# RWKV state step of a hybrid layer: both units' preparation at the step's opening, the output's scaling queued half a step later

## The chip, the cores and the metric

The kernel runs on one NeuronCore of a Trainium2 chip. That core has TensorE (PE in the profile; its weight loads are PEld), VectorE (DVE), ScalarE (ACT), GpSimd (POOL) and SyncE (SP), each with an instruction queue of its own that is worked through in order, and DMA queues that move data between HBM and the on-chip memories. Here nearly all DMAs are issued from SP's queue. The metric is the device time of one execution in microseconds (us). Three runs of the kernel before gave 2098.55, 2103.36 and 2105.53 us; the median is 2103.36 us.

## The reference, cut to what matters

A residual layer over 2048 tokens of width 1024. The normed input is projected once; the projection feeds two branches. One is an RWKV7 recurrence with 8 heads of 64, the other a latent attention that keeps the 256 best keys of each query. Their outputs are concatenated, projected back and added to the input (the measured layer closes with one more rmsnorm). The part that the change touches is the RWKV branch:

```python
def step(S, inp):                      # per token, 8 heads, state S is 64 x 64
    r_t, w_t, k_t, v_t, kk_t, a_t = inp
    sa = einsum('bhij,bhj->bhi', S, -kk_t)
    S = (S * w_t[:, :, None, :]
         + sa[..., None] * (kk_t * a_t)[:, :, None, :]
         + v_t[..., None] * k_t[:, :, None, :])
    return S, einsum('bhij,bhj->bhi', S, r_t)
...
y = rwkv7_scan(r, decay, k, v, kk, a)
mu = mean(y, -1); var = mean(square(y - mu), -1)
y = (y - mu) * rsqrt(var + GN_EPS) * gn_g + gn_b
y = y + sum(r * k * r_k, -1) * v
return y * silu(gate)
```

## The kernel before

The program has three parts in time. Up to about 1000 us the input is projected and the 256 keys of each query are found. Then the RWKV recurrence (`phase_r`, called R here) and the attention (T, lines 1221 to 1329) run beside each other. Last comes the output projection (W, lines 1362 to 1390). Every engine's order is fixed at build time by a scheduler that simulates a time line and always takes the ready instruction of the best priority: the chain of R has the highest, what stands in `with e.later()` a lower one, T lower still, W the lowest. `tc.issue_after(ins)`, in R through `behind(ins)`, puts the instructions of a block that run on the engine of `ins` behind `ins` in that engine's queue.

R works through 16 steps n of 128 tokens, each of two halves (o = 0 and 1) of 64 tokens. For one step there are two units i of four heads each. What a step needs is made two steps ahead and passes through these stages:

- `prep(n, i)`: the load `ld<-d_rw` (L937), a scan and products on DVE (L950 to L967), ACT exponentials, 16 small matmuls on PE (L974), masked into tile E by DVE (L977), the sum r*k*r_k on PE (L982) and its product with v, tile `bv`, on DVE (L984; eight buffers). POOL scales BK (L987).
- `systems`: from E of both units four stores to DRAM (`du<-E`, L1015, two from each unit) and one load of 512 KB that repeats the result over the partitions (`A<-du`, L1017). Tile A has one buffer.
- `inverse`: on POOL, Xr is set (L1025, L1027), and 31 pairs of operations (L1031 Xtmp, L1033 Xr) invert the small triangular systems in A; then a store `dx<-Xr` (L1034) and four loads `TT<-dx` (L1038; two buffers).
- `prep2`: PE transposes and ACT copies (L996 to L1006).
- `chain(n, o)`: PE reads the state with X and E (L1051, L1059), solves with TT (L1068, L1086), makes the state's change (L1093); DVE adds it into the state S (L1096), DVE makes SP, the decayed state (L1080), and ACT copies y (L1097).
- `tail_norm`: mean and variance of y in tile gst (DVE L1104 to L1111, ACT L1109), the reciprocal root as a `pow` on POOL (L1112), and the product of y with it on DVE (L1113, "the scale" below).
- `tail_out`: PE transposes y (L1120), ACT scales it into yo (L1126), POOL adds bv and multiplies by the gate gr (L1128, L1129), and yo is stored (L1130).

In step n the program opens with the inverse of step n+1, whose last L1033 is called `first`; then the norm of step n-1's y, its pow queued behind `first`; then unit 0's preparation for step n+2, its DVE work behind S of the half before; then chain half 0; then `prep2`, unit 1's preparation behind S of half 0, and `systems` for step n+2; then chain half 1 and the `tail_out` of step n-1. The scheduler fills the gaps with the matmuls, exponentials and masks of T.

Of the kernel before, what the change touches and what calls it, by code (L numbers as in the profile page):

```python
# [14 lines left out]
OP = mybir.AluOpType  # L15
# [871 lines left out]
def phase_r(env):  # L887


    e = NS(env)  # L890
    nc, tc, pa, ps, dma, V, S, G, PE, f32, rpow, nm, ident = (
        e.nc, e.tc, e.pr, e.psr, e.dma, e.V, e.S, e.G, e.PE, e.f32, e.rpow, e.nm, e.ident)
# [3 lines left out]
    NU = 2 * NC  # L896
# [4 lines left out]
    def tl(shape, dt, tag, bufs=1):  # L901
        return pa.tile(shape, dt, name=nm(tag), tag=tag, bufs=bufs)
# [105 lines left out]
    def systems(us):  # L1008

        du = e.dram([2, 2, NU, 32, 32], F32, nm("du"))  # L1010
        A = tl([128, 32, 32], F32, "A")
        for i, u in enumerate(us):
            for k in range(2):
                ps_ = slice(64 * i + k * 32, 64 * i + k * 32 + 32)
                dma(du[i, k].rearrange("u s t -> s u t"),  # L1015
                    u.E[ps_, :, :, k * 32:k * 32 + 32].rearrange("s h c t -> s (h c) t"))
        dma(A.rearrange("l s t -> l (s t)"),  # L1017
            du.rearrange("i k u s t -> (i k u) (s t)")[None].to_broadcast([4, 32, 1024]))
        return A

    def inverse(A):

        dx = e.dram([2, 2, NU, 32, 32], F32, nm("dx"))
        Xr = tl([128, 8, 32], F32, "Xr")
        G.memset(Xr, 0.0)  # L1025
        for j in range(4):
            G.memset(Xr.rearrange("p i t -> p (i t)")[32 * j:32 * j + 32, j:256:36], 1.0)  # L1027
        tmp = tl([128, 8, 32], F32, "Xtmp")
        for s in range(31):
            m, w = s // 4 + 1, 31 - s  # L1030
            G.tensor_tensor(tmp[:, :m, :w], Xr[:, :m, s:s + 1].to_broadcast([128, m, w]),  # L1031
                            A[:, s:s + 1, s + 1:].to_broadcast([128, m, w]), op=OP.mult)
            m_ = G.tensor_tensor(Xr[:, :m, s + 1:], Xr[:, :m, s + 1:], tmp[:, :m, :w], op=OP.add)  # L1033
        dma(dx.rearrange("i k u (r j) t -> j (i k u) r t", j=4), Xr)  # L1034
        TT = tl([128, NU, 32], F32, "TT", 2)
        for i in range(2):
            for k in range(2):
                dma(TT[Q[2 * i + k]], dx[i, k].rearrange("u s t -> s u t"))  # L1038
        return TT, m_.ins
# [60 lines left out]
    def tail_norm(y):  # L1100

        yv = y.rearrange("t c (h i) -> t (c h) i", h=2)
        st = tl([128, 3, NU], F32, "gst", 2)
        V.tensor_reduce(st[:, 0], yv, axis=AX.X, op=OP.add)  # L1104
        V.tensor_scalar(st[:, 0], st[:, 0], 1.0 / 64, None, op0=OP.mult)
        bc = lambda a: a[:, :, None].to_broadcast([128, NU, 64])
        V.tensor_tensor(yv, yv, bc(st[:, 0]), op=OP.subtract)
        sq = tl([128, NU, 64], F32, "ysq")
        S.activation(sq, yv, AF.Square)  # L1109
        V.tensor_reduce(st[:, 1], sq, axis=AX.X, op=OP.add)  # L1110
        V.tensor_scalar(st[:, 1], st[:, 1], 1.0 / 64, 64e-5, op0=OP.mult, op1=OP.add)  # L1111
        m = G.tensor_tensor(st[:, 2], st[:, 1], e.mhalf[:, :NU], op=OP.pow)  # L1112
        V.tensor_tensor(yv, yv, bc(st[:, 2]), op=OP.mult)  # L1113
        return m.ins

    def tail_out(us, y):

# [20 lines left out]
    def behind(ins):  # L1138
        return tc.issue_after(ins) if ins else ExitStack()

    def begin(n):
        return NS(dict(n=n, eC=tl([128, 2, NC], F32, "eC", 4), us=[]))
# [4 lines left out]
    first = G.memset(eLs[0][:, :, 0:1], 1.0).ins  # L1147
# [10 lines left out]
    y0, b0, state = None, None, None  # L1158
    for n in range(N):
        b = batch.pop(n)  # L1160
        new = batch[n + 2] = begin(n + 2) if n + 2 < N else None
        nx = batch.get(n + 1)
        with e.later():
            if nx:
                nx.TT, first = inverse(nx.A)
            if b0:
                with behind(first):
                    tail_norm(y0)
            if new:
                with behind(state):  # L1170
                    new.us.append(prep(n + 2, 0, new.eC, first))
        y = tl([128, NC, 128], F32, "y", 2)
        state = chain(b.us, b.TT, b.eC, y, n, 0)
        with e.later():
            if nx:
                for u in nx.us:
                    prep2(u)
            if new:
                with behind(state):
                    new.us.append(prep(n + 2, 1, new.eC, first))  # L1180
                new.A = systems(new.us)
        state = chain(b.us, b.TT, b.eC, y, n, 1)
        with e.later():
            if b0:
                tail_out(b0.us, y0)
        y0, b0 = y, b
    with e.later():
        tail_norm(y0)
        tail_out(b0.us, y0)


# [228 lines left out]
```

## Time and profile before

| | |
|---|---|
| median of three runs | 2103.36 us (2098.55 to 2105.53) |
| profiled execution | 2104.7 us, of which the span of the trace is 2102.9 us |
| mean granted clock of TensorE | 0.906 |
| busy: PE, DVE, ACT, POOL | 1803.3, 1296.7, 1019.8, 795.3 us |
| HBM traffic | 262.50 MB, 125 GB/s on average |

The three parts have different limits, so shares over the whole span say little. What is read below are stretches: from 1091 to 1730 us R and T run together, then R ends, and from 1830 us there is only T and then W. The stretches of the window rows are cut at the moments at which an inverse on POOL ends, so each of them is one turn of R.

### The profile page before, as it was taken

What the parts mean: (1) busy time and instruction counts of PE and PEld (TensorE: products, weight loads), DVE (VectorE), ACT (ScalarE), POOL (GpSimd) and SP (SyncE); (2) the same over time, 40 slices, a digit from 0 to 9 for tenths busy, and PEclk for the clock granted to TensorE, in tenths of its full rate; (3) what the DMA queues carried; (4) which work ended last, traced back from release to release, by engine and by line L of the source; (5) the groups of instructions that cost most, each with busy time, mean ns of one, the idle gap of its engine ahead of it and who ended that gap; (6) DMA issues with size and microseconds to landing.
All of it is one profiled execution on the core that took longest, in us unless ns stands there. A gap on an engine that the chain in (4) does not pass through costs nothing.

```text
span 2102.9 us, 36153 instructions
## 1 busy us (share of the span) xinstructions
PE 1803.3 (86%) x12906; PEld 1421.8 (68%) x12906; DVE 1296.7 (62%) x3050; ACT 1019.8 (48%) x1966; POOL 795.3 (38%) x1925
## 2 busy tenths in 40 slices
PE   5788998879796988986788988886988889899998
PEld 4666877658575867765566766665766667587776
DVE  5532538979779698986656557564756654644432
ACT  4422494453444744441355555454655567643431
POOL 1110124353544354562445645654546650100000
PEclk9778999989798999998799998798988899999999
DMA  7526334332262434234844355343454324744223
GB/s 248 199 94 200 108 101 135 101 115 85 75 239 63 135 107 136 91 95 125 204 102 105 95 136 147 105 119 98 115 143 131 93 78 108 233 128 128 66 93 112
DMA packets 309038, 262.50 MB, mean 125 GB/s; under 512 B 82544, under 2 KB 258288, under 8 KB 307696
## 3 DMA queue, kind: packets, MB, share of 16 engines
q1 hardware_dynamic: 304464, 248.03, 40.1%
q0 software_dynamic: 4384, 12.06, 1.8%
q8 instruction: 104, 1.70, 0.4%
q14 instruction: 86, 0.70, 0.1%
HBM read 166.37 MB, written 97.85 MB: 126 GB/s over the span
## 4 chain that ended last, share of the span: by engine, by line
PE 23%; POOL 14%; DMA 12%; issue 5%; DVE 4%; SPq 1%; ACT 1%; POOLq 0%; DVEq 0%; ACTq 0%
DMA A<-du 6%; POOL Xr L1033 6%; POOL Xtmp L1031 5%; PE om L1304 3%; PE po L1381 3%; PE po L1382 3%; PE po L1384 3%; PE tr L1295 3%; DMA dx<-Xr 2%; PE s L1261 2%; PE s L1262 1%; DMA TT<-dx 1%; DMA ld<-d_rw 1%; POOL yo L1129 1%; POOL gst L1112 1%
## 5 line engine op out<-in xcount | busy, mean ns | idle before, releaser
L577 PE MATMUL pm<-xh,wh 128*128 128x512 f32 x800 | 330.4, 414 | 20.3 <-DVE t L588 11.8
L578 PE MATMUL pm<-xl,wh 128*128 128x512 f32 x800 | 327.0, 409 | 0.0
L579 PE MATMUL pm<-xh,wl 128*128 128x512 f32 x800 | 326.1, 408 | 0.0
L1263 DVE CUSTOM_DVE_ANT_0 sc<-s,mk 128x512 f32<-128x512 f32 (+3 forms) x320 | 187.9, 607 | 102.8 <-PE s L1262 76.0
L1297 ACT ACTIVATE pt<-tr 128x512 f32<-128x512 f32 (+1 forms) x288 | 157.9, 569 | 160.8 <-PE tr L1295 115.9
L1031 POOL TENSOR_TENSOR Xtmp<-Xr,A 128x60 f32<-128x60 f32 (+24 forms) x496 | 146.9, 296 | 225.8 <-DMA A<-du 181.8
L577 PEld LDWEIGHTS pm<-xh,wh 128*128 128x128 f32 x800 | 158.1, 198 | 61.7 <-DVE t L588 13.7
L1270 ACT ACTIVATE sc<-sc,mx 128x128 f32<-128x128 f32 (+15 forms) x128 | 153.0, 1198 | 63.0 <-DVE mx L1269 62.7
L1295 PE MATMUL tr<-ident,sc 128*128 128x128 f32 x1088 | 180.1, 292 | 3.0 <-ACT pt L1297 2.6
L579 PEld LDWEIGHTS pm<-xh,wl 128*128 128x128 f32 x800 | 157.3, 197 | 36.4
L578 PEld LDWEIGHTS pm<-xl,wh 128*128 128x128 f32 x800 | 158.0, 197 | 35.4
L1304 PE MATMUL om<-pt,vt 128*64 128x128 f32 x2176 | 174.0, 295 | 6.2 <-DVE ga L1287 6.2
L1261 PE MATMUL s<-kt,q 128*128 128x512 f32 (+2 forms) x320 | 144.2, 454 | 35.8 <-DVE mx L1263 32.2
L1033 POOL TENSOR_TENSOR Xr<-Xr,Xtmp 128x60 f32<-128x60 f32 (+24 forms) x496 | 151.3, 305 | 37.4
L1304 PEld LDWEIGHTS om<-pt,vt 128*64 128x64 f32 x2176 | 134.2, 146 | 37.6 <-issue 19.6
L1295 PEld LDWEIGHTS tr<-ident,sc 128*128 128x128 f32 x1088 | 133.5, 149 | 33.9 <-issue 11.4
L317 ACT ACTIVATE mk<-x,st 128x1920 bf16<-128x1920 f16 (+5 forms) x72 | 98.0, 1361 | 103.6 <-POOL st L314 103.6
L249 ACT ACTIVATE rl<-lg,wi 128x512 f32<-128x512 f32 (+3 forms) x152 | 94.0, 631 | 99.6 <-PE lg L247 53.1
L1262 PE MATMUL s<-kt,q 128*128 128x512 f32 (+2 forms) x320 | 123.3, 389 | 8.1 <-DMA q<-d_q 8.0
L320 DVE TENSOR_SCALAR_CACHE_REDUCE mk<-x,st 128x2048 bf16<-128x2048 f16 (+5 forms) x72 | 120.6, 1675 | 1.4
L254 DVE SCALAR_TENSOR_TENSOR xs<-rl,wi,xs 128x512 f32<-128x512 f32 (+3 forms) x108 | 73.5, 681 | 60.9 <-ACT rl L249 60.1
L1387 POOL TENSOR_TENSOR st<-st 128x1 f32<-128x1 f32 x16 | 3.1, 195 | 277.1 <-ACT po L1386 277.1
(329 smaller groups left out, 3937.7 us busy)
## 6 DMA issues: line engine op xcount, KB each, us to landing
wraw<-in_w_in_dram SPq DMA_DIRECT2D x42, 512.0 KB
d_rw<-t SPq DMA_DIRECT2D x80, 256.0 KB
ld<-d_rw SPq DMA_DIRECT2D x32, 640.0 KB
q<-d_q SPq DMA_DIRECT2D x128, 128.0 KB
d_q<-t SPq DMA_DIRECT2D x32, 256.0 KB
d_kt<-t SPq DMA_DIRECT2D x32, 256.0 KB
kt<-d_kt SPq DMA_DIRECT2D x32, 256.0 KB
A<-du SPq DMA_DIRECT2D x16, 512.0 KB
```

The costliest lines, as they stand in the source:

```text
L577: PE.matmul(pm, wh[:, k], XH[g][:, k], start=k == 0, stop=False)
L578: PE.matmul(pm, wh[:, k], XL[g][:, k], start=False, stop=False)
L579: PE.matmul(pm, wl[:, k], XH[g][:, k], start=False, stop=k == KD - 1)
L1031: G.tensor_tensor(tmp[:, :m, :w], Xr[:, :m, s:s + 1].to_broadcast([128, m, w]), A[:, s:s + 1, s + 1:].to_broadcast([128, m, w]), op=OP.mult)
L1033: m_ = G.tensor_tensor(Xr[:, :m, s + 1:], Xr[:, :m, s + 1:], tmp[:, :m, :w], op=OP.add)
L1261: PE.matmul(pS[:, :wp], qh[:, h, qs], k[:, h, :wp], start=True, stop=False)
L1262: PE.matmul(pS[:, :wp], ql[:, h, qs], k[:, h, :wp], start=False, stop=True)
L1263: V.tensor_tensor_reduce(out=rows[h][:, c0:c0 + w], in0=pS[:, :w], in1=mk[:, c0:c0 + w], scale=1.0, scalar=LOW, op0=OP.add, op1=OP.max, ac ...
L1270: marks[p, b] = S.activation(rows[h][:, :n], rows[h][:, :n], AF.Exp, bias=mx[:, h, 4:5], accum_out=sums[:, h:h + 1]).ins
L1295: PE.transpose(pt[:, i, h], rows[h][:, (kb + i) * 128:(kb + i) * 128 + 128], ident)
L1297: S.activation(w[:, :m], pt[:, :m], AF.Copy)
L1304: PE.matmul(po[HALF[h]], v[:, (kb + i) % 4, HALF[h]], w[:, i, h], start=kb + i == 0, stop=kb + i == b)
```

## The change

The preparation of both units for step n+2 and its `systems` are now written at the step's opening, both behind S of the half before; unit 1 stood behind S of half 0 until now. `tail_norm` returns its last operation, the scale, without running it; the scale is written after chain half 0 and queued on DVE behind that half's S. The pow is the same operation on the same engine, behind the same instruction, called through a helper (`rpow`). No operation is added or removed, and the arithmetic is the same.

```diff
@@ -1109,9 +1109,8 @@
         S.activation(sq, yv, AF.Square)
         V.tensor_reduce(st[:, 1], sq, axis=AX.X, op=OP.add)
         V.tensor_scalar(st[:, 1], st[:, 1], 1.0 / 64, 64e-5, op0=OP.mult, op1=OP.add)
-        m = G.tensor_tensor(st[:, 2], st[:, 1], e.mhalf[:, :NU], op=OP.pow)
-        V.tensor_tensor(yv, yv, bc(st[:, 2]), op=OP.mult)
-        return m.ins
+        rpow(st[:, 2], st[:, 1])
+        return lambda: V.tensor_tensor(yv, yv, bc(st[:, 2]), op=OP.mult)
 
     def tail_out(us, y):
 
@@ -1165,27 +1164,28 @@
                 nx.TT, first = inverse(nx.A)
             if b0:
                 with behind(first):
-                    tail_norm(y0)
+                    scale = tail_norm(y0)
             if new:
-                with behind(state):
-                    new.us.append(prep(n + 2, 0, new.eC, first))
+                for i in range(2):
+                    with behind(state):
+                        new.us.append(prep(n + 2, i, new.eC, first))
+                new.A = systems(new.us)
         y = tl([128, NC, 128], F32, "y", 2)
         state = chain(b.us, b.TT, b.eC, y, n, 0)
         with e.later():
+            if b0:
+                with behind(state):
+                    scale()
             if nx:
                 for u in nx.us:
                     prep2(u)
-            if new:
-                with behind(state):
-                    new.us.append(prep(n + 2, 1, new.eC, first))
-                new.A = systems(new.us)
         state = chain(b.us, b.TT, b.eC, y, n, 1)
         with e.later():
             if b0:
                 tail_out(b0.us, y0)
         y0, b0 = y, b
     with e.later():
-        tail_norm(y0)
+        tail_norm(y0)()
         tail_out(b0.us, y0)
 
 
```

Since the scheduler sets the order from these priorities, the change moves rows on all engines. Three places of the two built programs are shown; a row is line, operation, output<-inputs with the numbers of the buffers, and the shape.

First place: step 3, on DVE, around the S of its half 0 (`S_1345`). SP_9430 belongs to half 1, y and gst to step 2's norm; ld, BK, X and E belong to unit 1 for step 5. Before:

```order
L1096 TENSOR_TENSOR S_1345_7771<-ch_9315,SP_9282 64x4x64 x2
L950 SCALAR_TENSOR_TENSOR L_9372<-restart_7748,ld_9368 128x256
L959 TENSOR_TENSOR BK_9378<-ld_9368 128x4x64
L962 TENSOR_SCALAR ka_9380<-ld_9368,kac,oka 128x128 x2
L1080 TENSOR_TENSOR SP_9430<-S_1345_7771,eC_8399 64x256 x2
L1280 TENSOR_TENSOR rs_15052<-sums_14898,rs_15052 128x2
L963 TENSOR_TENSOR ld_9368<-ld_9368,ka_9380 128x256
L966 TENSOR_TENSOR X_9377<-ld_9368,eL_1347_7775 128x4x64
L967 TENSOR_TENSOR X_9377<-ld_9368,eL_1347_7775 128x4x64
L1113 TENSOR_TENSOR y_8896<-y_8896,gst_9216 128x512
...
L977 TENSOR_TENSOR E_9388<-rp_9389,mask_7751 128x512
L977 TENSOR_TENSOR E_9388<-rp_9390,mask_7751 128x512
```

The same place after:

```order
L1096 TENSOR_TENSOR S_1345_7771<-ch_9361,SP_9328 64x4x64 x2
L977 TENSOR_TENSOR E_9285<-rp_9286,mask_7751 128x512
L1269 TENSOR_REDUCE mx_14897<-mx_14897 128x1
L1080 TENSOR_TENSOR SP_9430<-S_1345_7771,eC_8399 64x256 x2
L1113 TENSOR_TENSOR y_8942<-y_8942,gst_9216 128x512
L977 TENSOR_TENSOR E_9285<-rp_9287,mask_7751 128x512
L984 TENSOR_TENSOR bv_9302<-rp_9300,vt_9266 128x256
```

Unit 1's scan and products stood between S and the scale and its E far behind the scale; now they all stand ahead of S, except the second half of E, which stands right behind the scale.

The same step on SP, from the store dx of the inverse for step 4 to the load A for step 5 (the two du are unit 1's). Before:

```order
L1034 DMA dx_9140<-Xr_9141 4x256x32
L1038 DMA TT_9211<-dx_9140 32x8x32 x4
L941 DMA vt_9739<-d_v 128x2x192
L1329 DMA d_y<-ga_14633 128x128
L1221 DMA kt_15387<-d_kt_68 64x2x512
L1221 DMA kt_15387<-d_kt_69 64x2x512
L1244 DMA ga_15305<-d_ga 128x128
L1015 DMA du_9408<-E_9388 32x8x32 x2
L1221 DMA kt_15662<-d_kt_68 64x2x512
L937 DMA ld_9738<-d_rw 128x10x128
L1017 DMA A_9409<-du_9408 128x1x1024
```

The same place after:

```order
L1034 DMA dx_9140<-Xr_9141 4x256x32
L1242 DMA mk_15176<-d_mask_72 128x256
L1038 DMA TT_9211<-dx_9140 32x8x32 x4
L1015 DMA du_9305<-E_9285 32x8x32 x2
L937 DMA ld_9635<-d_rw 128x10x128
L1017 DMA A_9306<-du_9305 128x1x1024
```

A still stands behind TT and behind the du of unit 1, but fewer loads of T stand in between.

Second place: SP around the load A for step 7 (A_10149 before, A_10046 after) and the TT of step 6 (dx_9880, TT_9951). Before:

```order
L1015 DMA du_10148<-E_10128 32x8x32 x2
L1034 DMA dx_9880<-Xr_9881 4x256x32
L937 DMA ld_10478<-d_rw 128x10x128
L1017 DMA A_10149<-du_10148 128x1x1024
L1038 DMA TT_9951<-dx_9880 32x8x32 x4
```

The same place after:

```order
L1034 DMA dx_9880<-Xr_9881 4x256x32
...
L1038 DMA TT_9951<-dx_9880 32x8x32 x4
L1015 DMA du_10045<-E_9985 32x8x32
L937 DMA ld_10335<-d_rw 128x10x128
L1232 DMA q_2764_15667<-d_q_66 64x2x256
L1232 DMA q_2765_15670<-d_q_67 64x2x256 x2
L1329 DMA d_y<-ga_15178 128x128
L1242 DMA mk_15673<-d_mask_79 128x1152
L1244 DMA ga_15520<-d_ga 128x128
L1015 DMA du_10045<-E_10025 32x8x32 x2
L937 DMA ld_10375<-d_rw 128x10x128
L1017 DMA A_10046<-du_10045 128x1x1024
```

A stood ahead of TT and now stands behind TT, unit 1's du, two ld and five other entries.

Third place: POOL within the inverse for step 4 (A_9039 before, A_8936 after), where the yo of step 1 is finished. Before:

```order
L1031 TENSOR_TENSOR Xtmp_9147<-Xr_9141,A_9039 128x3x23
L1128 TENSOR_TENSOR yo_9123<-yo_9123,bv_8010 128x256
L1033 TENSOR_TENSOR Xr_9141<-Xr_9141,Xtmp_9147 128x3x23
L1128 TENSOR_TENSOR yo_9131<-yo_9131,bv_8050 128x256
L1129 TENSOR_TENSOR yo_9123<-yo_9123,gr_9124 128x256
L1031 TENSOR_TENSOR Xtmp_9147<-Xr_9141,A_9039 128x3x22
L1129 TENSOR_TENSOR yo_9131<-yo_9131,gr_9132 128x256
L1033 TENSOR_TENSOR Xr_9141<-Xr_9141,Xtmp_9147 128x3x22
```

The same place after:

```order
L1031 TENSOR_TENSOR Xtmp_9147<-Xr_9141,A_8936 128x5x14
L1127 TENSOR_TENSOR yo_9123<-yo_9123,bv_8010 128x256
L1033 TENSOR_TENSOR Xr_9141<-Xr_9141,Xtmp_9147 128x5x14
L1127 TENSOR_TENSOR yo_9131<-yo_9131,bv_8050 128x256
L1128 TENSOR_TENSOR yo_9123<-yo_9123,gr_9124 128x256
L1031 TENSOR_TENSOR Xtmp_9147<-Xr_9141,A_8936 128x5x13
L1128 TENSOR_TENSOR yo_9131<-yo_9131,gr_9132 128x256
L1033 TENSOR_TENSOR Xr_9141<-Xr_9141,Xtmp_9147 128x5x13
```

The four yo operations stood in the 9th and 10th pair of the 31 (width 23 and 22) and now stand in the 18th and 19th (width 14 and 13).

## Rows read from the trace of the kernel before

**Rows 1.** Page: the chain that ended last, by engine and by line.

```profile
PE 23%; POOL 14%; DMA 12%; issue 5%; DVE 4%; SPq 1%; ACT 1%; POOLq 0%; DVEq 0%; ACTq 0%
DMA A<-du 6%; POOL Xr L1033 6%; POOL Xtmp L1031 5%; PE om L1304 3%; PE po L1381 3%; PE po L1382 3%; PE po L1384 3%; PE tr L1295 3%; DMA dx<-Xr 2%; PE s L1261 2%; PE s L1262 1%; DMA TT<-dx 1%; DMA ld<-d_rw 1%; POOL yo L1129 1%; POOL gst L1112 1%
```

**Rows 2.** Waits, 1000 to 1820 us: total us, times, longest.

```profile
POOL Xtmp L1031 <- DMA A<-du: 181.8, 14, 18.6
...
DVE y L1113 <- POOL gst L1112: 74.0, 11, 15.6
...
PE ch L1068 <- DMA TT<-dx: 29.0, 5, 8.4
...
DVE bv L984 <- POOL yo L1128: 15.3, 5, 4.6
```

**Rows 3.** Windows: us, busy us of each engine, granted clock, DMA share.

```profile
1091.00:1730.60 639.60, 542.73 (x6260) 422.35 (x6258) 378.73 (x1159) 354.55 (x813) 357.60 (x1033) 0.89 0.44 114
1223.80:1276.50 52.70, 43.72 (x534) 33.68 (x534) 29.67 (x93) 28.02 (x69) 25.63 (x75) 0.93 0.57 149
1276.50:1322.90 46.40, 40.27 (x449) 30.51 (x450) 32.21 (x103) 26.58 (x69) 26.34 (x75) 0.82 0.50 134
1322.90:1363.40 40.50, 33.23 (x340) 26.90 (x338) 23.52 (x66) 17.93 (x43) 26.35 (x75) 0.75 0.41 106
1830.00:2045.00 215.00, 215.00 (x1365) 171.68 (x1365) 87.54 (x213) 87.49 (x166) 10.32 (x33) 0.99 0.34 106
```

**Rows 4.** Time line of SP, POOL, DVE after an inverse's end at 1276.5 us: start, us.

```profile
1281.26 1.80 SPq L1038 DMA_DIRECT2D TT<-dx  x4
1283.10 0.94 SPq L1015 DMA_DIRECT2D du<-E  x2
...
1285.50 0.74 SPq L1017 DMA_DIRECT2D A<-du  x1
...
1276.44 1.66 POOL L1112 TENSOR_TENSOR gst<-gst,mhalf 128x8 f32<-128x8 f32 x1
...
1296.28 0.40 POOL L1031 TENSOR_TENSOR Xtmp<-Xr,A 128x31 f32<-128x31 f32 x1 [13.15 <-DMA A<-du]
...
1278.13 1.52 DVE L1113 TENSOR_TENSOR y<-y,gst 128x512 f32<-128x512 f32 x1 [7.50 <-POOL gst L1112]
1279.57 0.68 DVE L977 TENSOR_TENSOR E<-rp,mask 128x512 f32<-128x512 f32 x1
```

**Rows 5.** Time line of SP, POOL, DVE after the end at 1223.8 us.

```profile
1237.71 0.55 SPq L1017 DMA_DIRECT2D A<-du  x1
...
1250.71 0.24 POOL L1031 TENSOR_TENSOR Xtmp<-Xr,A 128x31 f32<-128x31 f32 x1 [16.65 <-DMA A<-du]
...
1232.78 1.29 DVE L977 TENSOR_TENSOR E<-rp,mask 128x512 f32<-128x512 f32 x2 [1.38 <-PE rp L974]
```

**Rows 6.** Time line of SP, POOL, PE after the end at 1363.4 us.

```profile
1366.45 3.84 SPq L1017 DMA_DIRECT2D A<-du  x1
...
1372.25 3.57 SPq L1038 DMA_DIRECT2D TT<-dx  x4
...
1381.86 0.24 POOL L1031 TENSOR_TENSOR Xtmp<-Xr,A 128x31 f32<-128x31 f32 x1 [8.61 <-DMA A<-du]
...
1383.51 1.32 PE L1068 MATMUL ch<-R,TT 32*32 32x64 f32 x16 [7.47 <-DMA TT<-dx]
```

**Rows 7.** Groups by line and form, POOL then PE, 1091 to 1730.6 us: busy, mean ns.

```profile
L1128 POOL TENSOR_TENSOR yo<-yo,bv 128x256 f32<-128x256 f32 x26 | 19.5, 750 | 1.2 <-POOL Xr L1027 1.2
...
L1304 PE MATMUL om<-pt,vt 128*64 128x128 f32 x1288 | 109.8, 301 | 4.1 <-DVE ga L1287 4.1
L1295 PE MATMUL tr<-ident,sc 128*128 128x128 f32 x644 | 108.4, 295 | 1.2 <-ACT pt L1297 1.2
L1261 PE MATMUL s<-kt,q 128*128 128x512 f32 x135 | 66.3, 491 | 19.2 <-DVE mx L1263 19.2
L1262 PE MATMUL s<-kt,q 128*128 128x512 f32 x136 | 56.6, 416 | 0.1
```

## The prediction, made before the change was run

> **What bounds the kernel now.** I read the chain that ended last first, because the change touches only R and the question is whether R is on it. It is [rows 1]: beside 23% PE it holds 14% POOL and 12% DMA, and the largest lines are the load of A (6%) and the two lines of the inverse (6% and 5%). So for part of the span the end is set by a turn through POOL and the DMAs, not by TensorE. The waits of that part say where the turn stands still [rows 2]: POOL waited 181.8 us in 14 places for A. The next thing that the change names, DVE before the scale, waited 74.0 us in 11 places for POOL's pow.
>
> The windows tell how much room there is [rows 3]. From 1091 to 1730.6 us there are 14 turns of R in 639.6 us, 45.7 us each; PE is busy for 542.7 of them, so 97 us are idle. From 1830 to 2045 us PE is busy for 215.00 of 215 us: what T has left by then is paid in full. A shorter turn therefore pays only so far as PE's idle 97 us are cut, and the end time is the work of PE plus the idle time that R forces on it.
>
> A turn is 26 us of inverse (some 23 us of its own and four yo operations of 0.75 us, 3 us [rows 7]) and a gap of about 20 us until the next A has landed. I cut the 14 gaps (from the end of one inverse to the first L1031 of the next) into three kinds, of which one each is shown. On time: the inverse ends at 1276.5 us, TT is issued at 1281.26, the du of unit 1 at 1283.10, A at 1285.50, and POOL goes on at 1296.28 us, a gap of 19.8 us [rows 4]; seven are of this kind, 19.4 us on average. Late E: unit 1's E comes on DVE only at 1232.78 us, so A is issued 13.9 us after the end at 1223.8 and the gap is 26.9 us [rows 5]; three, 26.8 us on average. Early A: A goes out ahead of TT, at 1366.45 us, the gap is 18.5 us, but PE then waits 7.47 us for TT [rows 6]; four, 16.4 us on average. Seven, three and four of these make 281.8 us.
>
> **The change part by part.** Nothing is added or removed; the sum is of places.
>
> *Both preparations at the opening.* Where E was late, unit 1's scan and products stood behind S of half 0 and partly behind the stalled scale; now they stand ahead of S. Only the second half of E comes right behind the scale, as in the on-time turn, where E started at 1279.57 us, 1.44 us after the scale, and A went out 6 us later [rows 4]. So the three late gaps should become on-time ones. In the new order A stands ahead of TT in four of the 14 gaps, as before. New sum: 10 x 19.4 + 4 x 16.4 = 259.6 us, that is **-22 us** against 281.8.
>
> *SP's queue.* The early A's now lie at the two ends of R, and those in the middle are all behind their TT. In front of some stand more entries than the on-time kind has: about 9 more for step 7's A, 7 for step 12's, 5 for step 13's, one or two for steps 4 and 10. An issue on SP takes 0.45 us (TT, four in 1.80) to 0.74 us (A) [rows 4]; with 0.6 us for some 25 entries it is **+15 us** (11 to 19). It is nothing if these entries have left before the du is ready, which the on-time gap speaks against: there A is issued 0.7 us behind its predecessors with no idle time in front.
>
> *The scale.* The DVE stall in front of it does not go. The pow stays behind the end of the inverse, and in the new order two to five rows lie between S and the scale, where 11 to 38 lay. DVE's stream from one scale to the next is the same work, so the stall of 74.0 us over 11 places [rows 2] stays about what it is, and only the chain slides later against POOL. Behind the waiting scale stand E's second half, bv and T's masked scores; PE waits for the last. Price: **0**, bounds -10 to +10, since the length of the stall is the slack of the turn, 45.7 us less what DVE and PE need.
>
> *The yo operations.* The scale of step n-1 is followed by PE's transposes, ACT's yo and POOL's four yo operations, which now lie in the 18th and 19th pair of the inverse. Work of PE between the scale and the transposes is some 21.5 us (16 to 26) by the prices of rows 7, so yo is ready about 31 us after the end of the last inverse; POOL gets there at about 19.4 + 13 = 32.5 us. It just fits, and in the fuller turns it is 1 to 8 us late. I take **+5 us** for 14 turns (0 to +26). DVE's bv, which waits for an old yo to free its buffer, had 15.3 us of waits [rows 2] and goes with it.
>
> *Work of T inside R.* The scheduler believes that the new R is shorter and puts less of T into it. Counted in the order up to chain half 30, it is 5 pairs of score matmuls, 18 transposes and 26 value matmuls less. With 0.91 us a pair (491 + 416 ns), 0.168 us a transpose (108.4 / 644) and 0.17 us a value matmul (two records each, 109.8 / 1288) [rows 7] that is 4.6 + 3.0 + 4.4 = 12.0 us; at the last half 4.7 us. I take **+10 us** (5 to 13): this work is done later, where PE has no idle time [rows 3], and R is not shorter for it as long as POOL sets its pace.
>
> Sum: -22 + 15 + 0 + 5 + 10 = **+8 us**. The profiled execution took 2104.7 us, 1.3 us over the median of 2103.36; against the median the sum gives **2111 us**.
>
> **The rivals.** *A: the gain stays.* The late gaps are cured and SP's extra entries leave while DVE still works on E, so that they cost nothing; the yo operations fit. For it: the three long turns are the plainest loss in the windows, 52.7 us against 40.5 to 46.4 for the next two [rows 3]. Against it: the extra entries stand in the built order. The sum is then -22 to -27 (the waits of PE for TT, 29.0 us in 5 places [rows 2], shrink too) and 0 to +5: 2080 to 2086, say **2083 us**.
>
> *B: a loop over POOL and DVE, slower.* Scale, transposes, yo, the rest of the inverse, pow, next scale form a ring. If PE's stream from the scale to the transposes takes over 29 us rather than 21.5, every inverse stops in its 18th pair and its end, TT and pow all move. With the middle turns 2 us late each this adds 26 us in place of 5, less some that the A gap hides: +22 us or **2125 us**. For it: PE is 85% busy here, and its granted clock drops to 0.75 in single turns [rows 3]. Against it: the transposes' operands are early.
>
> *C: nothing moves.* All four terms are shifts of work against a turn that has some 5 us of slack; they cancel to within a few microseconds: **2103 us** (2099 to 2108).
>
> *D: the stall really goes.* If the half step were enough for the pow to be done when DVE comes to the scale, up to 74.0 us of DVE's waiting were freed. DVE is not what sets the turn (378.7 of 639.6 us busy [rows 3]), so at most about half would reach PE: **2070 us**. It needs the pow to run earlier, and that is still behind the inverse.
>
> *E: A's load hidden.* In the rows, A is issued 9.0 us after the end of one inverse and waited for to the last, 13.15 us of POOL standing still [rows 4]. If the earlier preparation let A go out during the inverse before, the gaps would vanish and with them most of PE's 97 us: 2104 - 97, **2006 us**. Against it: A has one buffer, which the running inverse reads to its last pair.
>
> The Trainium skill's page "DMA: Bandwidth & Descriptors" (Rules for kernel authors) asks for E's state of things: issue a DMA early, compute, wait late, so that its fixed cost overlaps. By that rule the change should gain; the trace shows the transfer fully exposed, and with one buffer it stays so.
>
> **How the numbers follow.** The forecast (2103 to 2117) gets 0.42, half of it within 0.3% of the median, which is 2097.0 to 2109.7 us and about what a measurement of this kernel can tell from no change. A gets 0.22, B 0.20, C 0.10, D 0.04, E 0.02. Faster is A, D and E: 0.28. Slower is B and over half of the forecast, 0.42. The rest, 0.30, is no change. The range of 8 in 10 runs from 2080 (most of A) to 2131 us (B with half its bound more); D and E and the edges of A and B stay out. Cases of both signs hold much of it; the likeliest one's own range is 2103 to 2117 us.
>
> **What would show it.** In the profile after: A issued within about 10 us of each inverse's end and no gap over 24 us shows the first step right; a total wait for A near 160 + 15 us shows the second; a wait of DVE for the pow still of 50 to 90 us the third (near zero: D); waits of POOL in mid-inverse for ACT's yo, 0 to 26 us, the fourth (over 1.5 us in most turns: B); PE idle in the 14 turns near 105 us and T further behind at the end of R the fifth. The forecast is wrong if the turn falls to 44 us or less (A) or rises over 47 us (B), or if PE's idle time no longer follows POOL's turn.

## The result, and the profile after

The changed kernel takes 2132.6 us (median of 4 runs, 2128.3 to 2135.6) against 2101.0 us (4 runs, 2097.7 to 2105.5) of the kernel before: a ratio of 1.0148, with a 95% interval of 1.013 to 1.0166. It is slower, as forecast, but by 31.6 us where +8 us were forecast, and it lies 1.6 us above the range. In the two profiled runs the difference is 31.0 us; these are taken apart below.

First the windows of the kernel after (columns as in [rows 3]): the same 14 turns, from the end of one inverse to the end of the 14th behind it, and all that follows.

```profile
1085.60:1743.70 658.10, 546.04 (x6108) 424.27 (x6104) 386.43 (x1137) 349.77 (x803) 371.71 (x1032) 0.87 0.43 109
1743.70:2133.90 390.20, 366.18 (x2634) 288.92 (x2632) 166.91 (x438) 177.73 (x354) 28.28 (x64) 0.96 0.40 121
```

The 14 turns start 5.4 us earlier than before (1091.0 us), take 658.1 us instead of 639.6 [rows 3], and what follows takes 390.2 us. What follows them in the kernel before:

```profile
1730.60:2102.90 372.30, 348.80 (x2452) 276.15 (x2452) 159.74 (x412) 167.05 (x335) 28.91 (x64) 0.97 0.40 123
```

So -5.4 + 18.5 + 17.9 = 31.0 us, the whole difference of the spans (2133.9 and 2102.9 us). The loss has two halves: longer turns, and more work of PE left behind them (366.2 us busy instead of 348.8).

The second half can be counted. Score matmuls, transposes and value matmuls of T from 1000 us to the end of the 14th turn, line by line, first before, then after:

```profile
L1261 PE MATMUL s<-kt,q x220: 274/476/882, 1001.8 to 1724.6; 128*128 128x512 f32 x77, 128*128 128x256 f32 x22, 128*128 128x384 f32 x11
L1295 PE MATMUL tr<-ident,sc x716: 270/273/476, 1002.8 to 1725.8; 128*128 128x128 f32 x179
L1304 PE MATMUL om<-pt,vt x1400: 272/273/476, 1013.1 to 1721.2; 128*64 128x128 f32 x175
```

```profile
L1261 PE MATMUL s<-kt,q x209: 279/478/881, 1001.9 to 1743.2; 128*128 128x512 f32 x74, 128*128 128x256 f32 x20, 128*128 128x384 f32 x11
L1295 PE MATMUL tr<-ident,sc x683: 269/273/477, 1000.9 to 1742.8; 128*128 128x128 f32 x171
L1304 PE MATMUL om<-pt,vt x1352: 272/273/477, 1008.8 to 1742.2; 128*64 128x128 f32 x194
```

11 pairs of score matmuls at 0.91 us, 33 transposes at 0.168 and 48 records of value matmuls (two make one matmul) at 0.085 [rows 7] are 19.6 us of work less, although R took longer.

The first half: cut as in the prediction, the 14 gaps are 284.4 us (before 281.7) and the 14 inverses 373.7 us (before 357.9). So 15.8 of the 18.5 us are in the inverse itself. Its two lines, busy time and mean length, before and then after:

```profile
L1033 POOL TENSOR_TENSOR Xr<-Xr,Xtmp 128x60 f32<-128x60 f32 (+24 forms) x435 | 132.8, 305 | 32.6
L1031 POOL TENSOR_TENSOR Xtmp<-Xr,A 128x60 f32<-128x60 f32 (+24 forms) x434 | 128.1, 295 | 202.5 <-DMA A<-du 163.2 <-DMA TT<-dx 7.8
```

```profile
L1033 POOL TENSOR_TENSOR Xr<-Xr,Xtmp 128x60 f32<-128x60 f32 (+24 forms) x435 | 137.9, 317 | 32.6
L1031 POOL TENSOR_TENSOR Xtmp<-Xr,A 128x60 f32<-128x60 f32 (+24 forms) x434 | 135.1, 311 | 203.6 <-DMA A<-du 172.1
```

The same operations on the same shapes are 12 and 16 ns longer, 12.1 us in sum; the four yo operations of each turn add 2.3 us (40.7 us against 38.4). The time line of POOL, then of DVE, in one inverse after shows when: the first L1033 takes 0.74 us while DVE runs L1107, the second 0.71 us while it runs L950; the L1031 between them, beside L1263, takes 0.27 us, and without DVE beside it an L1033 of 52 elements takes 0.28 us.

```profile
1682.62 0.74 POOL L1033 TENSOR_TENSOR Xr<-Xr,Xtmp 128x52 f32<-128x52 f32 x1
1683.44 0.27 POOL L1031 TENSOR_TENSOR Xtmp<-Xr,A 128x50 f32<-128x50 f32 x1
1683.79 0.71 POOL L1033 TENSOR_TENSOR Xr<-Xr,Xtmp 128x50 f32<-128x50 f32 x1
```

```profile
1682.54 0.68 DVE L1107 TENSOR_TENSOR y<-y,gst 128x512 f32<-128x512 f32 x1
1683.15 0.68 DVE L1263 CUSTOM_DVE_ANT_0 sc<-s,mk 128x512 f32<-128x512 f32 x1
...
1683.76 0.68 DVE L950 TENSOR_TENSOR_SCAN L<-restart,ld 128x256 f32<-128x256 f32 x1
```

Over all L1031 and L1033 of the 14 turns, what each is longer than the shortest of its shape in the same kernel adds up to 19.1 us before and 32.7 us after. Operations with nothing of DVE beside them carry 1.4 and 0.9 us of it (399 and 313 operations). The rest, shared out among the DVE operations beside them by the length of the overlap, is per us of overlap 0.36 to 0.44 us with L950, 0.5 with L1107, 0.2 to 0.3 with the products of `prep` (L959 to L967, without L962), and 0.02 to 0.05 with L1263 and L977, whose first input is in PSUM. Unit 1's scan and products used to run partly in the gaps, while POOL stood waiting for A; now both units' run mostly beside the inverse: the scans and products lie beside L1031 and L1033 for 57.1 us in the 14 turns, before 36.6 us, and L1107 for 8.5 us, before 1.9.

Last, the queue of SP (its waits over the same 14 turns): the rows of the yo store, L1130 before and L1129 after, and above them the longest row, T's load of ga (L1244).

```profile
SPq L1244 <- DMA d_y<-ga: 103.4, 32, 9.5
...
SPq L1130 <- POOL Xtmp L1031: 34.0, 14, 11.1
...
SPq L1130 <- POOL Xr L1033: 22.5, 12, 5.9
```

```profile
SPq L1244 <- DMA d_y<-ga: 97.8, 26, 10.3
SPq L1129 <- POOL Xtmp L1031: 56.0, 11, 17.5
SPq L1129 <- POOL Xr L1033: 43.4, 10, 14.6
SPq L1129 <- POOL yo L1128: 38.6, 5, 11.2
```

SP stands 138 us in front of these stores and waits for POOL, before 56.5 us, because yo is now made in the 16th to 22nd pair of the inverse in 11 of 13 turns, before mostly in the 1st to 11th. All that is queued behind them waits too: T's loads, ld, du. The wait for ga is about as long in both kernels; what is queued behind it differs.

### The profile page after: what moved, and what is told of

Same layout as the page of the kernel before. It is cut to its first block, busy times and chain, and to the rows that moved or that the text cites. A ratio compares the mean times of both kernels' runs of the same rounds, so it can differ in the third digit from the quotient of the medians.

```text
span 2133.9 us, 36172 instructions
## 1 busy us (share of the span) xinstructions
PE 1817.5 (85%) x12906; PEld 1431.1 (67%) x12906; DVE 1311.8 (61%) x3050; ACT 1021.5 (48%) x1966; POOL 810.0 (38%) x1925
## 4 chain that ended last, share of the span: by engine, by line
PE 21%; POOL 15%; DMA 13%; issue 4%; DVE 3%; SPq 2%; ACT 1%; POOLq 0%; DVEq 0%; ACTq 0%
POOL Xr L1033 6%; POOL Xtmp L1031 6%; DMA A<-du 6%; PE om L1304 3%; PE po L1384 3%; PE tr L1295 3%; PE po L1381 3%; PE po L1382 3%; DMA dx<-Xr 3%; PE s L1261 2%; PE s L1262 1%; DMA du<-E 1%; DMA ld<-d_rw 1%; POOL yo L1128 1%; DMA q<-d_q 1%
## 5 line engine op out<-in xcount | busy, mean ns | idle before, releaser
L1263 DVE CUSTOM_DVE_ANT_0 sc<-s,mk 128x512 f32<-128x512 f32 (+3 forms) x320 | 188.1, 605 | 129.8 <-PE s L1262 68.7
L1031 POOL TENSOR_TENSOR Xtmp<-Xr,A 128x60 f32<-128x60 f32 (+24 forms) x496 | 153.1, 309 | 226.7 <-DMA A<-du 190.4
L1261 PE MATMUL s<-kt,q 128*128 128x512 f32 (+2 forms) x320 | 147.4, 463 | 40.0 <-DVE mx L1263 34.9
L1033 POOL TENSOR_TENSOR Xr<-Xr,Xtmp 128x60 f32<-128x60 f32 (+24 forms) x496 | 156.7, 316 | 37.4
L1262 PE MATMUL s<-kt,q 128*128 128x512 f32 (+2 forms) x320 | 125.1, 394 | 11.7 <-DMA q<-d_q 11.7
```

Source lines behind the costliest of these rows:

```text
L1261: PE.matmul(pS[:, :wp], qh[:, h, qs], k[:, h, :wp], start=True, stop=False)
L1262: PE.matmul(pS[:, :wp], ql[:, h, qs], k[:, h, :wp], start=False, stop=True)
L1263: V.tensor_tensor_reduce(out=rows[h][:, c0:c0 + w], in0=pS[:, :w], in1=mk[:, c0:c0 + w], scale=1.0, scalar=LOW, op0=OP.add, op1=OP.max, ac ...
```

## The experiments

All times are medians of 4 to 12 runs beside the kernel before on the same chip, whose median there was 2098 to 2103 us. "Turns", "gaps" and "inverses" are the 14 turns cut as above, "tail" is the span behind them, transposes are the records of T's line of transposes up to their end, PE idle is the span less PE's busy time on the page. Of each edit the lines that carry it are shown; comments in them are added.

| kernel | us, ratio | turns = gaps + inverses | tail | transposes | PE idle |
|---|---|---|---|---|---|
| before | 2101, 1 | 639.6 = 281.7 + 357.9 | 372.3 | 716 | 299.6 |
| after | 2132.6, 1.0148 | 658.1 = 284.4 + 373.7 | 390.2 | 683 | 316.4 |
| part one alone | 2132.3, 1.0134 | 653.5 = 282.6 + 371.0 | 391.0 | 675 | 315.0 |
| part two alone | 2108.6, 1.0029 | 642.9 = 288.5 + 354.4 | 376.6 | 700 | 317.8 |
| stores behind dx | 2124.7, 1.0117 | 651.2 = 277.8 + 373.3 | 384.8 | 684 | 304.1 |
| E before scale | 2122.8, 1.0098 | 660.3 = 286.3 + 374.0 | 371.1 | 724 | 305.7 |
| SP free | 2126.6, 1.0141 | 645.3 = 273.5 + 371.9 | 395.2 | 676 | 311.1 |
| A before TT | 2119.2, 1.0107 | 631.2 = 254.2 + 376.9 | 394.9 | 674 | 290.2 |
| A first, SP free | 2096.6, 0.9992 | 618.5 = 244.0 + 374.6 | 393.5 | 658 | 277.1 |
| the same, no part two | 2101.3, 1.0016 | 619.8 = 246.7 + 373.1 | 395.2 | 665 | 280.9 |
| before, SP free | 2095.2, 0.9976 | 659.8 = 307.1 + 352.6 | 351.0 | 766 | 295.8 |
| before, behind A | 2095.3, 0.9959 | 661.7 = 302.3 + 359.4 | 343.1 | 774 | 305.0 |

The turn sums are single profiled executions and the scheduler rearranges T in each kernel, so differences of a few us in one column mean nothing; the interval of a ratio is given where it decides. The profiled run of "before, SP free" (2102.0 us) is the longest of its ten, that of "part two alone" (2113.1 us) the second longest.

**Which part costs.** Part one alone:

```
             if new:
-                with behind(state):
-                    new.us.append(prep(n + 2, 0, new.eC, first))
+                for i in range(2):
+                    with behind(state):
+                        new.us.append(prep(n + 2, i, new.eC, first))
+                new.A = systems(new.us)
```

> Part one alone: both units' preparation at the opening, the scale left behind the pow as before. In the built order the four yo operations stand in the 17th to 21st pair of the inverse as in the changed kernel, but unit 1's E no longer stands behind the scale in most turns. If the loss comes from the preparation's new place (yo late in the inverse, less of T inside R): 2125 to 2140 us, like the changed kernel. If it comes from the scale that is queued ahead of E (theory: PE waits for E and bv, 45.6 us in the changed kernel against 20.8 before): 2095 to 2110 us.

2132.3 us, ratio 1.0098 to 1.0171. The place of the preparation alone costs all that the change costs. PE waits 50.9 us for E and bv there too, although the scale was not moved.

Part two alone, the scale behind S of half 0 with the preparation as before:

```
             if b0:
+                with behind(state):
+                    scale()
```

> Part two alone: the scale queued behind S of half 0, the preparation as before. Its built order is that of the kernel before in the first seven turns, and yo stays in the first 12 pairs. If the loss comes from the preparation's new place: 2098 to 2110 us, no change. If it comes from the late scale itself: 2120 to 2135 us. T has 13.6 us less work inside R up to half 30 by the order, so up to +13 us is open even then.

2108.6 us, ratio 1.0012 to 1.0046: a loss that is small but clear of noise (6 us by the ratio, 7.9 by the medians), with the inverse at its old length (354.4 us) and less of T in R (700 transposes). In company with part one it adds nothing that can be measured.

**SP's queue.** First the stores alone, behind the store dx of the inverse in which yo is made:

```
+        with behind(stored[-1]):        # the DMA dx
+            for dst, yo in outs:
+                dma(dst, yo)
```

> The changed kernel with the two yo stores of each step queued on SP behind the store dx of the inverse in which yo is made; the orders of the other engines stay nearly the same. Theory of SP's queue: the stores hold SP for 138 us in the 14 turns against 64 us before, and the loads behind them come late; then this gives back 15 to 30 us (2103 to 2117 us) and SP's wait for yo is near 0. Theory of the E behind the scale, or of the inverse itself: within 5 us of the changed kernel, 2128 to 2138 us.

2124.7 us, ratio 1.0079 to 1.0155, some 8 us below the changed kernel, with intervals that overlap. It did not take the hold away, as the waits of SP show (L1123 is the load of gr):

```profile
SPq L1123 <- POOL Xtmp L1031: 72.4, 13, 17.4
SPq L1123 <- POOL Xr L1033: 68.9, 13, 14.7
```

The load of the gate gr for the next step waits for the same yo operations to free its buffer. So both were moved:

```
+            for u in us:
+                u.gr = tl([128, 2, W], F32, "gr", 2)
+                dma(u.gr, ...)           # behind dx as well
```

> The changed kernel with both the two yo stores and the two loads of gr, whose buffer is freed by the same yo operations, queued on SP behind the store dx. The earlier run moved the stores alone and the loads of gr then held SP for 141 us in the 14 turns, so SP's hold was not taken away there. Theory of SP's hold: here neither waits for POOL, T's loads come in time, and the time falls to 2108 to 2118 us. Against it: four more entries stand between dx and A in every turn, 2.4 us by 14 turns, 34 us at most; and if SP's hold costs nothing, 2125 to 2150 us.

2126.6 us, ratio 1.0105 to 1.0177. The turns fell by 13 us, the tail rose by 5. The interval overlaps that of the changed kernel (1.013 to 1.0166) almost wholly, and the expected 2108 to 2118 us did not come: SP's hold alone is not the cause of the loss.

**E behind the scale.**

```
-                with behind(state):
+                with behind(state), behind(new.us[1].made if new else state):   # made: unit 1's E
                     scale()
```

> The changed kernel with the scale queued behind unit 1's E on DVE too, so that no E stands behind the waiting scale. Theory of the E behind the scale: PE's waits for E and bv fall from 45.6 us to about 20, the time to 2105 to 2115 us; T has 16 us more work inside R up to half 30 by the order, which pulls the same way. Theory of SP's queue or of yo late in the inverse: no gain, 2128 to 2140 us, since yo stands as late or later.

2122.8 us, ratio 1.0069 to 1.0127: 10 us back. DVE's wait for the pow fell from 80.1 to 52.2 us, PE's for E and bv fell from 45.7 to 26.2 us in all, not quite to the expected 20. The longest rows are:

```profile
DVE y L1113 <- POOL gst L130: 52.2, 11, 7.8
...
DVE bv L984 <- POOL yo L1127: 31.7, 8, 8.1
PE rp L974 <- DVE bv L984: 10.9, 3, 5.1
PE rp L982 <- DVE E L977: 9.5, 7, 4.1
```

The turns did not get shorter (660.3 us); the 10 us come from T, whose 724 transposes and tail of 371.1 us are those of the kernel before. In most of these turns E is done 2 to 8 us before the inverse ends, and A still goes out 9 to 12 us after it.

**A behind TT.** In the changed kernel the longest gap is 27.0 us, from 1313.7 us. SP's time line there is the second place of the order shown ahead of the prediction:

```profile
1313.73 0.58 SPq L1034 DMA_DIRECT2D dx<-Xr  x1
1314.41 2.12 SPq L1232 DMA_DIRECT2D q<-d_q  x1
1316.58 1.00 SPq L1015 DMA_DIRECT2D du<-E  x1
1318.54 1.79 SPq L1038 DMA_DIRECT2D TT<-dx  x4
...
1324.22 0.43 SPq L1242 DMA_DIRECT2D mk<-d_mask  x1
1327.54 0.32 SPq L1244 DMA_DIRECT2D ga<-d_ga  x1
1327.96 0.88 SPq L1015 DMA_DIRECT2D du<-E  x2
1328.93 1.47 SPq L937 DMA_DIRECT2D ld<-d_rw  x1
1331.54 0.55 SPq L1017 DMA_DIRECT2D A<-du  x1
```

E was done at 1320.2 us, but unit 1's du stands behind a load ga of T that cannot go before 1327.5 us, and A 17.8 us after the end of the inverse. In the next run TT stands behind A, and the scale behind E:

```
-        TT = tl([128, NU, 32], F32, "TT", 2)   # in inverse(n + 1)
...
+            if nx:                              # after systems(n + 2)
+                with behind(new.us[0].sent if new else None):   # sent: the DMA A
+                    nx.TT = solved(dx)
```

> The changed kernel with the scale behind unit 1's E and the four loads TT queued on SP behind the load A. In the changed kernel E is done 4 to 10 us before the inverse ends in half of the turns, yet A goes out 9 to 12 us after it, because the order puts unit 1's du and A behind TT, and TT waits 4.7 us for dx to land. Theory that this order forfeits the gain: A goes out within 1 to 5 us, the gaps fall from 20 to 13 to 16 us as in the turns that had A first, the 14 turns from 658 to 590 to 620 us, and the time to 2070 to 2100 us. Theory that the turn is bound elsewhere (PE's work in a turn, TT late for the chain): the gaps fall, PE's wait for TT rises by as much, 2115 to 2135 us.

The gaps fell from 284.4 to 254.2 us and the turns to 631.2, 27 us shorter than in the changed kernel, and PE's wait for TT hardly rose (3.0 us against 2.4). A goes out 5 to 9 us after the end of the inverse in nine of the 14 turns, within 5 us in two. Yet the time is 2119.2 us, ratio 1.0067 to 1.0147, in the range of the second theory but not for its reason, and not clear of noise against the changed kernel (1.013 to 1.0166). This run contains the edit of the run before it, E before the scale, which has 1.0098 by itself. Against that run the turns are 29 us shorter and the end comes no earlier: the tail, 394.9 us, is 23.8 us longer, and 50 transposes fewer are done when it begins.

Then the stores and gr behind A as well, so that they neither hold SP nor stand in front of A:

> As the run with A ahead of TT, with the yo stores and the gr loads behind A as well, so that SP waits neither for yo nor for gr. If SP's hold and the order of A and TT both cost: 5 to 20 us below the run with A ahead of TT alone. If SP's hold costs nothing: within 5 us of it.

2096.6 us, ratio 0.9976 to 1.0009: the time of the kernel before again, and 22.6 us below the run with A ahead of TT on the same chip. Windows of this kernel, the turns and the tail:

```profile
1083.40:1701.90 618.50, 534.24 (x6022) 413.02 (x6017) 387.43 (x1122) 343.13 (x790) 374.60 (x1032) 0.90 0.44 115
1701.90:2095.40 393.50, 373.73 (x2721) 293.32 (x2720) 169.36 (x451) 181.40 (x366) 28.78 (x64) 0.98 0.40 121
```

R's turns end at 1701.9 us, 28.7 us earlier than in the kernel before, and the program ends 7.5 us earlier in the profile and not measurably earlier in the median. 58 transposes fewer were done by then, the tail is 21.2 us longer. So a faster turn does not pay by itself: it leaves the work of T for later. That these edits together make up the loss does not show that they undo its causes; they may be gains of their own.

Without part two, the same:

> The run with A first and SP free, without the second part of the change: the scale follows its pow in the program again. If the second part costs 8 us, as it did alone: 2085 to 2093 us. If the late scale behind unit 1's E was what gave that run its last gain: 2098 to 2110 us.

2101.3 us, ratio 0.9994 to 1.0038. The first expectation is excluded (no run was under 2097.4 us), the time lies in the second. The difference from the run with part two, 0.24%, is not clear: the intervals overlap. The loss of part two alone does not show here; with E in front, no harm of the late scale can be seen.

**The inverse beside DVE.** Two kernels add 16 products a step to the kernel before, from SBUF or from PSUM:

```
             V.tensor_tensor(u.E[:, h], pe[h], mk, op=OP.mult)
+            for _ in range(4):
+                V.tensor_tensor(fl(L), fl(u.E[:, h, 0:2]), fl(restart), op=OP.mult)   # or fl(pe[h][:, 0:2])
```

> The kernel before with 16 more products a step on DVE right behind the four E operations (256 elements a row, 0.42 us each, 6.7 us a step), with both inputs in SBUF; their result is not used. Theory that DVE's operations on SBUF slow POOL's inverse when they run beside it (in the trace of the changed kernel the L1031 and L1033 operations with such an operation beside them are longer by 0.2 to 0.5 us per us of overlap, those with a PSUM input beside them by 0.03): the mean of L1031 and L1033 rises from 295 and 305 ns to over 315. Theory that the inverse is longer for another reason: they stay within 5 ns.

> The same 16 extra products a step on DVE as in the run with inputs in SBUF, at the same place and of the same size, but with the first input in PSUM. Theory that it is DVE's work on SBUF inputs that slows POOL's inverse: the means of L1031 and L1033 stay near the kernel before (295 and 305 ns), below 303 and 311, where the SBUF run has 314 and 319. Theory that any extra DVE work beside the inverse, or the changed order, lengthens them: 312 ns and 317 ns or more.

Inverse lines of the SBUF kernel, then of the PSUM kernel, from 1090 to 1740 us (L1033 is Xtmp and L1035 Xr there):

```profile
L1035 POOL TENSOR_TENSOR Xr<-Xr,Xtmp 128x60 f32<-128x60 f32 (+24 forms) x425 | 135.7, 319 | 32.1
L1033 POOL TENSOR_TENSOR Xtmp<-Xr,A 128x60 f32<-128x60 f32 (+24 forms) x425 | 133.6, 314 | 201.7 <-DMA A<-du 170.6
```

```profile
L1035 POOL TENSOR_TENSOR Xr<-Xr,Xtmp 128x60 f32<-128x60 f32 (+24 forms) x412 | 127.0, 308 | 32.0
L1033 POOL TENSOR_TENSOR Xtmp<-Xr,A 128x60 f32<-128x60 f32 (+24 forms) x411 | 120.9, 294 | 223.9 <-DMA A<-du 193.2
```

319 and 314 ns with SBUF inputs, 308 and 294 with a PSUM input, 305 and 295 without the extra work (the 14 turns by themselves have 319 and 313, 306 and 294). The extra products lie beside the inverse's operations for 39.8 us with SBUF inputs and 25.0 us with a PSUM input; a joint fit over all DVE operations gives 0.40 and 0.02 us for each us. It is DVE's work with two inputs in SBUF that slows POOL, not DVE's being busy. The Trainium skill's page "GPSIMD Engine Reference" (1. Specifications) says that GpSimd shares its SBUF interfaces with VectorE and contends with VectorE instructions that have two SBUF inputs; the two runs agree, and here it is 0.2 to 0.5 us for each us of overlap.

The pair shows what lengthens the inverse, not what that costs: the 14 inverses are 366.0 us with SBUF inputs and 336.6 us with a PSUM input, and the two kernels take 2118.7 and 2116.1 us (one run each).

**A version that beats both.** The kernel before, with only the stores and the gr loads moved, first behind dx, then behind A:

> The kernel before, with the yo stores and the gr loads behind the store dx on SP, and nothing of the change. SP waits 56.5 us for yo there in the 14 turns. Theory that SP's hold costs in the order before too: 2085 to 2097 us; by the order 33 us more of T's work lies inside R up to half 30. Theory that it is only a cost of yo late in the inverse: 2096 to 2106 us, or a few us more for the entries between dx and A.

> The kernel before, with the yo stores and the gr loads queued on SP behind the load A of the step instead of behind dx, and nothing of the change. Against the run that put them behind dx (2095.2 us, ratio 0.9976) no entry of theirs stands between dx and A, and the order has as much of T inside R. Theory that the length of a turn sets the end: the gaps shrink by about 2 us in each of 14 turns, 2065 to 2080 us. Theory that the end is PE's work plus PE's idle time, whatever the turn: 2085 to 2097 us.

2095.2 us, ratio 0.9959 to 0.9992, and 2095.3 us, ratio 0.9941 to 0.9977, each beside the kernel before on its own chip; between the two no difference shows. The first lies in the range that was given for a cost of SP's hold, the second in the range that does not go by the length of a turn. The second is 0.4% faster than the kernel before, while its turns are 22 us longer:

```profile
1090.60:1752.30 661.70, 554.39 (x6456) 430.08 (x6453) 389.47 (x1201) 367.37 (x835) 357.31 (x1032) 0.90 0.44 112
1752.30:2095.40 343.10, 322.18 (x2255) 255.13 (x2251) 146.04 (x368) 152.89 (x311) 28.64 (x63) 0.99 0.42 131
```

Its R ends 21.7 us later than before, but 58 transposes more are done by then, and the tail is 29.2 us shorter. The end follows what PE has done, not when R is done. Not all of it is idle time, though: in this profile PE is busy for 12.9 us less than in the kernel before (1790.4 us) and idle for 5.4 us more. The changed kernel with all three repairs (0.9992) is not faster than this one (0.9959), which has the stores and gr behind A alone; so nothing here shows a gain from the preparation at the opening.

## Why the prediction was wrong in size

**What held.** The sign, for two of the reasons given: less of T inside R, and SP's queue giving back the cure of the late E. E is no longer later than 6.5 us after the end of an inverse, where three were 10 to 13 us late. POOL's total wait for A, 172.1 us, is near the sign given for it (175). The DVE stall in front of the scale stayed, as forecast: 80.1 us in 12 places against 74.0 in 11 [rows 2] (in the 14 turns by themselves 61.4 in 9 before). The yo operations fitted: in the 14 turns POOL did not wait for ACT's yo, so the +5 us did not come and rival B's ring did not occur, although a turn of 47.0 us is the length that was to tell of it. DVE's bv waited 16.4 us for yo (15.3 before). The two rows after:

```profile
DVE y L1113 <- POOL gst L130: 80.1, 12, 9.6
...
DVE bv L984 <- POOL yo L1127: 16.4, 6, 4.4
```

Rival E did not occur either. The rule of the Trainium skill's page "DMA: Bandwidth & Descriptors" (Rules for kernel authors), to issue a DMA early and wait for it late, could not be followed to the end here: with one buffer of A, even where the kernel with A in front of TT sends A 5 us after an inverse's end, POOL waits another 9 to 11 us for it.

**The inverse, missed.** The step that failed first is the term "both preparations at the opening". It counted what the moved work does to the gaps (-22 us) and took the inverse, "some 23 us of its own", as fixed: the inverse's own growth stood in the sum at nothing, without a reason. It was +15.8 us. DVE's 4 us of scan and products per unit were costed on DVE's queue alone, and what runs beside them was not asked. The rows that would have told it were in the trace of before: its L1031 and L1033 beside L950 or L1080 were longer by 0.35 us per us of overlap there too.

**The gaps, -22 + 15 = -7 forecast, +2.7 measured.** The order came as forecast, A ahead of TT in four of the 14 gaps, and these four are 13.8 us on average, shorter than the 16.4 put down for them. The ten with A behind TT are 22.9 us where 19.4, or 20.9 with the term for SP's queue, were forecast, 20 us in sum over the 20.9. In 10 of the 14 gaps E was ready at the latest 4 us after the end of the inverse, and still seven gaps are over 21 us and four over the 24 us given as a sign, since du and A wait behind TT and T's loads; single places cost up to 8 us (the ga load above), not 0.6 us an entry. I priced SP's entries by their issue and not by what the entry itself waits for.

**T inside R, +10 forecast, 19.6 us of work and a tail 17.9 us longer measured.** The direction and the cause are as forecast; counted up to S of half 0 of step 14, the order alone has 10.9 us less. The rest comes from the slide that I priced at nothing: DVE adds this S at 1744.7 us, 1 us behind the end of the 14th turn, where before it did so at 1719.1 us, 11.5 us ahead of that end. PE stands earlier in its order by that much when R's turns are over.

**SP's hold by the yo store.** It was not in the sum at all: 138 us of standing where 56.5 us were. Taking it away by itself gave nothing clear of noise (the run with SP free); with A and E in front as well it gave 22.6 us (2119.2 to 2096.6 us).

**PE's clock.** Of the 31 us, 14.2 are longer busy time of PE (1817.5 us against 1803.3) for the same matmuls, and 16.8 are longer idle time, 15 of them in the 14 turns (112.1 us, before 97; 105 was given as the sign). The granted clock of the 14 turns is 0.87 after and 0.89 before. Over a whole run it is 0.899 to 0.903 in the four runs of the changed kernel and 0.903 to 0.915, on average 0.909, in 62 runs of the kernel before. Whether the clock is a cause of the loss or comes with it is not shown, nor that it sets PE's busy time: the run with A before TT has 1825.2 us at 0.911. I had treated PE's work as constant.

**What stays open.** By the terms of the sum the 31.0 us are +15.8 for the inverse, +2.7 for the gaps, +17.9 for the tail and -5.4 for the earlier start. Which cause made how much of them cannot be read from these terms: each kernel has another order of T, and the effects do not add up. By the ratios E before the scale gives back 0.5%, A before TT on top of it nothing that can be measured, SP free by itself nothing clear of noise, all three 1.6%. The inverse's 16 us could not be taken away without moving the preparation back. They are still there (374.6 us) in the run that made up the loss, and in the pair with the extra products 29 us of inverse (beside gaps that differ the other way) went with 2.5 us at the end, so no run shows that they cost anything at the end. The run with A in front and SP free shows that they need not, if the gaps shrink by 40 us. The kernel before with A in front of TT was not run, so how much of that repair is a gain of its own stays open too.

## What to carry to other kernels

Before costing a reordering by waits and queues, ask which engines' work becomes simultaneous: two engines can slow each other where neither waits for the other, as DVE's scan and products slowed POOL's inverse by 0.2 to 0.5 us per us of overlap, and the trace of before shows the price in the spread of one instruction form. In an in-order DMA queue a store whose source is made late holds all loads behind it (138 us of standing here); place such a store, and the load that reuses its buffer, behind the work that is known to be done (0.2 to 0.4% in the kernel before). Where a background stream fills the gaps of a chain and is itself the end of the program, a shorter chain need not end it earlier: turns 21 us shorter gave no gain here, and turns 22 us longer with more of T done gave 0.4%. So count the background's progress and not the chain's end.

## What was not expected of the hardware

One POOL operation of 50 or 52 elements a row, 0.27 to 0.28 us alone, took 0.71 to 0.81 us beside a DVE subtraction (L1107) or scan (L950) with two SBUF inputs that itself takes about 0.68 us, and 0.27 to 0.28 us beside a DVE operation that reads PSUM. Of the two shown above, 0.60 and 0.64 us lie beside the DVE operation; by what is left of their 0.28 us, they went on there at a quarter to a third of their own pace (an estimate from these lengths).
